# Up-projection matmuls that read and write their 512 token columns in short alternating runs

## The chip, the cores and the metric

The kernel runs on one core of a Trainium2 chip. The metric is the device time of one execution in microseconds (us). Before the change, three timed runs gave a median of 1272.12 us (1269.15 to 1272.39).

## The reference, cut to what matters

Two layers of a small transformer trunk on 512 tokens with a model width of 1024. Layer 0 has stick-breaking attention, layer 1 forgetting attention, each with 16 heads of 64. Each layer ends in a gated channel mixer with 2 x 2816 hidden columns, and that is where the change lies. All arithmetic is float32:

```python
def conv_ffn(x, w_up, conv_w, conv_b, w_down):
    hdn = x @ w_up                                  # (512, 1024) @ (1024, 5632)
    hdn = lax.conv_general_dilated(                 # causal, depthwise, width 3, along the tokens
        hdn, conv_w[:, None, :], window_strides=(1,), padding=[(CONV_WIDTH - 1, 0)],
        dimension_numbers=('NWC', 'WIO', 'NWC'), feature_group_count=2 * D_FF) + conv_b
    gate, up = jnp.split(hdn, 2, axis=-1)
    return (jax.nn.gelu(gate, approximate=True) * up) @ w_down
...
    f = conv_ffn(rmsnorm(h, ffn_pre_g[layer]), w_up[layer], conv_w[layer],
                 conv_b[layer], w_down[layer])
    h = h + rmsnorm(f, ffn_post_g[layer])
```

## The kernel before, in words

**The number format.** Every float32 operand is split into a high part in TensorE's reduced float32 format (`hi`, `AH`) and the remainder (`lo`, `AL`). A product is three matmuls: high by high, high weights by low activations, low weights by high activations.

**Weights.** All weights come as tiles of 512 KB, in the order of one list, `stream`. `make` (L130 to L149) loads a tile by a DMA from SyncE's queue, rounds it on ScalarE (L144) and subtracts on VectorE in two halves (L148). `take` hands out the next tile and keeps `NW` = 8 tiles made ahead.

**The up-projection.** The normalised activations stand transposed in `AH` and `AL`: 128 partitions, 8 blocks of model columns (`KT`), 512 tokens. The 2816 hidden columns are 22 chunks (`NC`) of 128. For each chunk `c` the function `up` (inside `ffn_phase`) computes two products, the gate's half and the linear half, into the two banks of `pair_of(c)`, one of four pairs of PSUM banks. Each product is one call of `w_stationary`: 8 blocks x 3 matmuls = 24 matmuls that add into one bank, the weight tile as the stationary operand, 128 x 512 tokens as the moving one (L213). A chunk thus is 48 matmuls on TensorE.

**Order.** The first three chunks (`EARLY` = 3) run in two halves of 256 tokens each. Chunks 3 to 21 run one after the other with all 512 tokens, `up(c)` and then `gate(c)`. `gate` evacuates both banks: ScalarE's first term of the convolution, VectorE's two further terms (L589), the GELU on ScalarE (L594) and the product on VectorE (L595). After chunk 21 the down-projection (L513) follows. `w_stationary` serves the q, k and gate projections of the attention stages too, with the same line number. The order on the engines is made by the tile framework's scheduler when the program is built.

**Other lines that the rows below name.** All operands of TensorE's moving side and all its outputs are single stretches of columns in this kernel. Some VectorE operations are not. L662 and L666, once each in the set-up, reduce a 128 x 128 identity: L662 sums 16 groups of 8 elements that lie 16 elements apart (64 bytes), so each read is a jump; L666 sums 4 groups, each of 2 runs of 16 elements. L397 (`project_v`) reads PSUM in runs of 128 columns and writes runs of 64 with gaps of 64. L430 (a row maximum in the second attention) and L465 (a difference of a PSUM tile and its rounded copy) go through stretches without a gap.

The loop of a layer, and the matmul at its heart:

```python
for k in range(KT):
    for a, b in ((hi, AH), (hi, AL), (lo, AH)):
        nc.tensor.matmul(ps, a[:, k, :m], b[:, k, t0:t1], start=i == 0, stop=i == n - 1)
...
for c in range(EARLY, NC):
    up(c, (take(), take()), 0, T)
    gate(c)
```

Of the kernel before, what the change touches and what calls it, by code (L numbers as in the profile page):

```python
# [14 lines left out]
P = 128  # L15
T = 512
D = 1024
KT = D // P
# [7 lines left out]
NEG = -1.0e30  # L26
GUARD = 2.0**60
NW = 8
EARLY = 3
POOL_ROWS = (1, 5, 7)  # L30
FILL = (4, 5)
# [6 lines left out]
def f32(ap):  # L38
    return ap.bitcast(F32)
# [3 lines left out]
def tile_trunk(  # L43
# [22 lines left out]
    nc = tc.nc  # L66
# [12 lines left out]
    def pair_of(i):  # L79
        b = PAIRS[i % 4]  # L80
        return PS[:, b : b + 2, :]

    def bank(kind):
        b = {"pj": 4, "zt": 6}[kind] + turn[kind] % 2
        turn[kind] += 1
        return PS[:, b, :]
# [16 lines left out]
    AH = const.tile([P, KT, T], F32R, name="AH")  # L103
    AL = const.tile([P, KT, T], F32R, name="AL")
# [24 lines left out]
    def make(i):  # L129
        src, nk, n, g, eng = stream[i]  # L130
        raw = wp.tile([P, nk, n], F32, name=f"raw{i}", tag="raw", bufs=2)
        hi = wp.tile([P, nk, n], F32R, name=f"whi{i}", tag="whi", bufs=NW)
        lo = wp.tile([P, nk, n], F32R, name=f"wlo{i}", tag="wlo", bufs=NW)
        nc.sync.dma_start(raw, src)
# [19 lines left out]
    def ahead(n):  # L154
        while nmade[0] < min(len(stream), n):
            make(nmade[0])
            nmade[0] += 1

    def take():
        i = nused[0]  # L160
        nused[0] += 1
        ahead(i + NW)
        return made.pop(i)
# [32 lines left out]
    def act_table(name):  # L196
        with ExitStack() as stack:
            for i in users[-8:]:
                stack.enter_context(tc.issue_after(i))
            ld = nc.scalar.preload_act_table_set(name)  # L200
        return tc.issue_after(ins(ld))

    def uses_table(i):
        users.append(ins(i))


    def w_stationary(ps, w, t0=0, t1=T, m=P):
        hi, lo = w
        n = 3 * KT
        i = 0  # L210
        for k in range(KT):
            for a, b in ((hi, AH), (hi, AL), (lo, AH)):
                nc.tensor.matmul(ps, a[:, k, :m], b[:, k, t0:t1], start=i == 0, stop=i == n - 1)  # L213
                i += 1
# [8 lines left out]
    def pre_block(b, g, t4, junk):  # L223

        ss = small.tile([P, 4], F32, name="ss")
        nc.scalar.activation(junk, H[:, b, :], AF.Square, accum_out=ss[:, 0:1])  # L226
        r = rstd_of(ss)
        if g is None:
            nc.scalar.activation(t4, H[:, b, :], AF.Copy, scale=r)
        else:  # L230
            nc.vector.scalar_tensor_tensor(out=t4, in0=H[:, b, :], scalar=r, in1=g, op0=ALU.mult, op1=ALU.mult)  # L231
        ps = pair_of(b).rearrange("p a (k c) -> p (a k) c", c=P)
        for k in range(KT):
            nc.tensor.transpose(ps[:, k, :], t4[:, k * P : (k + 1) * P], ident)  # L234
        sl = slice(b * P, (b + 1) * P)
        nc.scalar.copy(AH[:, :, sl], ps)
        nc.vector.tensor_tensor(out=AL[:, :, sl], in0=ps, in1=f32(AH[:, :, sl]), op=ALU.subtract)

    def post_block(b, y, g, t4, junk):

        ss = small.tile([P, 4], F32, name="ss")
        nc.scalar.activation(junk, y, AF.Square, accum_out=ss[:, 0:1])  # L242
        nc.vector.tensor_tensor(out=t4, in0=y, in1=g, op=ALU.mult)  # L243
        r = rstd_of(ss)
        nc.vector.scalar_tensor_tensor(  # L245
            out=H[:, b, :], in0=t4, scalar=r, in1=H[:, b, :], op0=ALU.mult, op1=ALU.add
        )
# [19 lines left out]
    def gain(pool, g):  # L267
        t = pool.tile([P, D], F32, name="g", tag="g", bufs=2)
        nc.sync.dma_start(t, g.rearrange("(o d) -> o d", o=1).broadcast_to([P, D]))
        return t  # L270


    class Attn:
# [19 lines left out]
        def gates(self):  # L293
# [17 lines left out]
            for t0 in (0, T // 2):  # L311
                w_stationary(ps[:, t0 : t0 + T // 2], ws, t0, t0 + T // 2)
# [206 lines left out]
    def flat_pair(i):  # L519
        return pair_of(i).rearrange("p a c -> p (a c)")  # L520

    def out_proj(done, heads_end):

        w = {}
        after = []
        one = [(1, k) for k in range(KT)]
        order = [(0, k) for k in range(KT - 2)] + one[: FILL[0]] + [(0, KT - 2), heads_end[0]]
        order += one[FILL[0] : FILL[1]] + [heads_end[1]] + one[FILL[1] :]
        order += [(0, KT - 1)] + [(b, k) for b in (2, 3) for k in range(KT)]
        for step in order:  # L530
            if not isinstance(step, tuple):
                after.append(step)
                continue
            b, k = step
            if k not in w:
                w[k] = take()
            with ExitStack() as stack:
                for i in after:
                    stack.enter_context(tc.issue_after(i))
                after = [unit(b, k, KT, (AH[:, k, :], AL[:, k, :]), w[k])]  # L540
            if k == KT - 1:
                done(b)
# [19 lines left out]
    def ffn_phase(l, heads_end, post_g, next_g, final):  # L562
        with tc.tile_pool(name=f"ffn{l}", bufs=2) as pool:
            g1 = gain(pool, post_g)
            g2 = gain(pool, ffn_pre_g[l])
            junk = pool.tile([P, D], mybir.dt.bfloat16, name="junk", bufs=1)

            def mixed(b):
                t4 = pool.tile([P, D], F32, name="t4", tag="t4", bufs=3)
                post_block(b, flat_pair(b), g1, t4, junk)  # L570
                pre_block(b, g2, t4, junk)

            out_proj(mixed, heads_end)
            act = pool.tile([P, NC, T], F32, name="act", bufs=1)

            def up(c, w, t0, t1):
                for i in range(2):
                    w_stationary(pair_of(c)[:, i, t0:t1], w[i], t0, t1)

            def gate(c):  # L580
                y = pair_of(c)
                hc2 = pool.tile([P, 2, T], F32, name="hc", tag="t4", bufs=3)
                hs = []
                for i in range(2):
                    col = cw[:, l, :].rearrange("p (w c) -> p w c", w=4)[:, :, i * NC + c]
                    hc = hc2[:, i, :]
                    nc.scalar.activation(hc, y[:, i, :], AF.Identity, scale=col[:, 2:3], bias=col[:, 3:4])
                    for s in (1, 2):
                        nc.vector.scalar_tensor_tensor(  # L589
                            out=hc[:, s:], in0=y[:, i, : T - s], scalar=col[:, 2 - s : 3 - s], in1=hc[:, s:],  # L590
                            op0=ALU.mult, op1=ALU.add,
                        )
                    hs.append(hc)
                uses_table(nc.scalar.activation(hs[0], hs[0], AF.Gelu_apprx_tanh))  # L594
                nc.vector.tensor_tensor(out=act[:, c, :], in0=hs[0], in1=hs[1], op=ALU.mult)  # L595

            with act_table("gelu_apprx_tanh_and_others"):
                ws = [(take(), take()) for _ in range(EARLY)]
                for t0 in (0, T // 2):
                    for c in range(EARLY):  # L600
                        up(c, ws[c], t0, t0 + T // 2)
                for c in range(EARLY):
# [5 lines that stand above are left out]
            def lhs(k):  # L608
                ah = pool.tile([P, T], F32R, name="ah", bufs=4)
                al = pool.tile([P, T], F32R, name="al", bufs=4)  # L610
                nc.scalar.copy(ah, act[:, k, :])  # L611
                nc.vector.tensor_tensor(out=al, in0=act[:, k, :], in1=f32(ah), op=ALU.subtract)  # L612
                return ah, al

            g3 = gain(pool, ffn_post_g[l])

            def fed(b):
                t4 = pool.tile([P, D], F32, name="t4", tag="t4", bufs=3)
                if final and b == NB - 1:
                    finish(b, pair_of(b), g3, t4, junk)  # L620
                    return
                post_block(b, flat_pair(b), g3, t4, junk)
                if final:
                    nc.sync.dma_start(of[:, b, :], H[:, b, :])
                else:
                    pre_block(b, next_g, t4, junk)

            down_proj(lhs, fed, final)


    with tc.tile_pool(name="pre", bufs=2) as pool:
# [12 lines left out]
        for l in range(2):  # L644
            rows = [conv_w[l, w].rearrange("(c p) -> c p", p=P) for w in range(3)]
            rows.append(conv_b[l].rearrange("(c p) -> c p", p=P))
            for i in range(2):
# [3 lines left out]
                ps = bank("zt")[:, : 2 * nb]  # L651
# [5 lines left out]
        ps = bank("zt")[:, : 2 * KT]  # L657
# [53 lines left out]
```

## Time and profile before

| what | value |
|---|---|
| median of three timed runs | 1272.12 us (1269.15 to 1272.39) |
| the profiled execution's own time | 1275.83 us |
| its span, first to last instruction | 1274.1 us |
| TensorE busy | 1234.1 us, 97% of the span, 6485 matmuls |
| TensorE weight loads busy | 1062.4 us, 83% |
| VectorE busy | 810.5 us, 64% |
| ScalarE busy | 644.7 us, 51% |
| GpSimd busy | 101.7 us, 8% |
| mean granted TensorE clock | 0.991 of full speed |
| DMA | 111.97 MB, mean 88 GB/s |

"Busy" is the share of the span in which an engine had an instruction in flight. Matmuls are pipelined and the profile models their ends, so one matmul's duration overlaps the next one's; what a matmul costs in a stream is the distance from its start to the next start. Weight loads are listed apart from matmuls and run beside them.

### The profile page before, as it was taken

Reading aid. Unit: us, or ns where it says so; the run is one execution under the profiler, and the core shown is the slowest. Engines: PE = TensorE matmul, PEld = TensorE weight load, DVE = VectorE, ACT = ScalarE, POOL = GpSimd, SP = SyncE. Lnnn points to the kernel's source line nnn. Section 1 sums busy time; section 2 is a strip of 40 time slices with the busy share of each in tenths; the row PEclk is TensorE's granted clock in tenths of the full one; section 3 lists DMA queues with packets and bytes.
Section 4 is the critical chain, followed back from the end, with each engine's and each line's share of the span. In section 5 each row is a group of like instructions: output and inputs, shape, how many; then the busy total and the mean of one; then the engine's idle time right before and its main releaser. Section 6 shows DMA issues by size and latency. Waiting matters only on the chain. (4 is left out here: it accounts for less than half of the span.)

```text
span 1274.1 us, 16820 instructions
## 1 busy us (share of the span) xinstructions
PE 1234.1 (97%) x6485; PEld 1062.4 (83%) x6485; DVE 810.5 (64%) x1304; ACT 644.7 (51%) x1085; POOL 101.7 (8%) x163
## 2 busy tenths in 40 slices
PE   6999998999999999999999999999999999999998
PEld 6888886789888888888888988977898888888886
DVE  6899898676655555433477887774775555554323
ACT  5767677445433333323488787664554333333221
POOL 1000003020000000000001222341100000000001
PEclk9999999999999999999999999999999999999999
DMA  6421212034333333333233122110443333333311
GB/s 215 139 66 51 66 50 67 25 90 143 107 99 99 99 93 93 97 99 100 67 81 88 50 83 67 50 50 34 146 120 100 99 99 99 94 93 96 99 34 66
DMA packets 145928, 111.97 MB, mean 88 GB/s; under 512 B 4680, under 2 KB 136120, under 8 KB 145848
## 3 DMA queue, kind: packets, MB, share of 16 engines
q1 hardware_dynamic: 145848, 110.90, 29.4%
q8 instruction: 51, 0.84, 0.3%
q14 instruction: 29, 0.24, 0.1%
HBM read 108.79 MB, written 2.10 MB: 87 GB/s over the span
## 5 line engine op out<-in xcount | busy, mean ns | idle before, releaser
L213 PE MATMUL PS<-AH,whi 128*128 128x512 f32 (+1 forms) x1088 | 398.8, 367 | 4.3 <-DVE QS L362 2.8
L213 PE MATMUL PS<-AL,whi 128*128 128x512 f32 (+1 forms) x1088 | 398.0, 366 | 0.0
L213 PE MATMUL PS<-AH,wlo 128*128 128x512 f32 (+1 forms) x1088 | 397.8, 366 | 0.0
L148 DVE TENSOR_TENSOR wlo<-raw,whi 128x512 fp32r<-128x512 f32 x332 | 217.4, 697 | 211.7 <-ACT whi L144 211.0
L144 ACT CAST whi<-raw 128x1024 fp32r<-128x1024 f32 x172 | 180.8, 1052 | 223.5 <-PE PS L213 177.7
L213 PEld LDWEIGHTS PS<-AH,whi 128*128 128x128 f32 x1088 | 205.6, 189 | 37.2 <-DVE QS L362 3.4
L213 PEld LDWEIGHTS PS<-AL,whi 128*128 128x128 f32 x1088 | 205.8, 189 | 31.8
L213 PEld LDWEIGHTS PS<-AH,wlo 128*128 128x128 f32 x1088 | 205.8, 189 | 31.8
L589 DVE SCALAR_TENSOR_TENSOR hc<-PS,cw,hc 128x511 f32<-128x511 f32 (+1 forms) x176 | 130.7, 745 | 2.7
L513 PE MATMUL PS<-whi,ah 128*128 128x512 f32 x352 | 109.4, 389 | 0.0
L513 PE MATMUL PS<-wlo,ah 128*128 128x512 f32 x352 | 109.4, 389 | 0.0
L513 PE MATMUL PS<-whi,al 128*128 128x512 f32 x352 | 109.4, 389 | 0.0
L612 DVE TENSOR_TENSOR al<-act,ah 128x512 fp32r<-128x512 f32 x44 | 30.4, 690 | 117.2 <-ACT ah L611 117.2
L611 ACT CAST ah<-act 128x512 fp32r<-128x512 f32 x44 | 27.4, 622 | 144.3 <-PE PS L513 138.2
L391 PE MATMUL PS<-whi,AH 128*128 128x256 f32 x256 | 74.9, 293 | 3.9 <-DVE QS L362 1.6
L513 PEld LDWEIGHTS PS<-wlo,ah 128*128 128x128 f32 x352 | 66.1, 188 | 13.8
L513 PEld LDWEIGHTS PS<-whi,ah 128*128 128x128 f32 x352 | 66.1, 188 | 13.7
L219 POOL TENSOR_SCALAR ss<-ss 128x1 f32<-128x1 f32 x31 | 11.9, 385 | 821.0 <-ACT junk L242 755.2
L513 PEld LDWEIGHTS PS<-whi,al 128*128 128x128 f32 x352 | 66.1, 188 | 13.6
L391 PE MATMUL PS<-wlo,AH 128*128 128x256 f32 x256 | 74.6, 291 | 0.0
L391 PE MATMUL PS<-whi,AL 128*128 128x256 f32 x256 | 74.2, 290 | 0.0
L594 ACT ACTIVATE hc<-hc 128x512 f32<-128x512 f32 x44 | 27.8, 631 | 86.8 <-DVE hc L589 86.8
(130 smaller groups left out, 1766.3 us busy)
## 6 DMA issues: line engine op xcount, KB each, us to landing
raw<-w_up_dram SPq DMA_DIRECT2D x88, 512.0 KB
raw<-w_down_dram SPq DMA_DIRECT2D x44, 512.0 KB
raw<-sb_w_qkv_dram SPq DMA_DIRECT2D x24, 512.0 KB
raw<-w_kvf_dram SPq DMA_DIRECT2D x16, 512.0 KB
raw<-sb_w_o_dram SPq DMA_DIRECT2D x8, 512.0 KB
raw<-fox_w_q_dram SPq DMA_DIRECT2D x8, 512.0 KB
raw<-fox_w_o_dram SPq DMA_DIRECT2D x8, 512.0 KB
H<-x_dram SPq DMA_DIRECT2D x4, 512.0 KB
```

The lines of the kernel that those rows point to most:

```text
L144: nc.scalar.copy(hi, raw)
L148: eng.tensor_tensor(out=fl[:, s], in0=fr[:, s], in1=fh[:, s], op=ALU.subtract)
L213: nc.tensor.matmul(ps, a[:, k, :m], b[:, k, t0:t1], start=i == 0, stop=i == n - 1)
L219: nc.gpsimd.tensor_scalar(ss[:, 2:3], ss[:, 0:1], 1.0 / D, EPS, op0=ALU.mult, op1=ALU.add)
L391: nc.tensor.matmul(ps[:, o], a[:, k, sl], m[:, k % 4, :], start=i == 0, stop=i == 3 * KT - 1)
L513: mm = nc.tensor.matmul(y[:, c, :], s[:, sl], m[:, 0, c * 512 : (c + 1) * 512], start=k == 0 and i == 0, stop=k == n - 1 and i == 2,)
L589: nc.vector.scalar_tensor_tensor(out=hc[:, s:], in0=y[:, i, : T - s], scalar=col[:, 2 - s : 3 - s], in1=hc[:, s:], op0=ALU.mult, op1=ALU.add,)
L594: uses_table(nc.scalar.activation(hs[0], hs[0], AF.Gelu_apprx_tanh))
L611: nc.scalar.copy(ah, act[:, k, :])
L612: nc.vector.tensor_tensor(out=al, in0=act[:, k, :], in1=f32(ah), op=ALU.subtract)
```

## The change

For chunks 3 to 21 of both layers, a matmul of the up-projection goes through its 512 token columns in another order. The columns 0 to 255 and 256 to 511 are the two halves. `woven` makes a view that takes `run` columns of the first half, `run` columns of the second, the next `run` of the first, and so on. The same view is put on the moving operand and on the output in PSUM, so each token's result lands where it stood before. The run depends on the chunk's number modulo 8:

| chunk mod 8 | 0 | 1 | 2 | 3 | 4 | 5 | 6 | 7 |
|---|---|---|---|---|---|---|---|---|
| run, columns | none (as before) | 128 | 64 | 32 | 16 | 8 | 4 | 2 |
| chunks | 8, 16 | 9, 17 | 10, 18 | 3, 11, 19 | 4, 12, 20 | 5, 13, 21 | 6, 14 | 7, 15 |
| matmuls in both layers | 192 | 192 | 192 | 288 | 288 | 288 | 192 | 192 |
| runs in one matmul | 1 | 4 | 8 | 16 | 32 | 64 | 128 | 256 |

No instruction is added, taken away or moved: the order on all five engines, the waits among them and the number of instructions are those of the kernel before, and TensorE's list differs in the shape of 1632 matmuls alone (a matmul of chunk 3 is 128x8x2x32 where it was 128x512).

```diff
+RUNS = (None, 128, 64, 32, 16, 8, 4, 2)
...
-    def w_stationary(ps, w, t0=0, t1=T, m=P):
+    def woven(ap, run):
+
+        return ap.rearrange("p (h j c) -> p j h c", h=2, c=run)
+
+    def w_stationary(ps, w, t0=0, t1=T, m=P, run=None):
         hi, lo = w
+        if run:
+            n = 3 * KT
+            i = 0
+            for k in range(KT):
+                for a, b in ((hi, AH), (hi, AL), (lo, AH)):
+                    nc.tensor.matmul(
+                        woven(ps, run), a[:, k, :m], woven(b[:, k, t0:t1], run), start=i == 0, stop=i == n - 1
+                    )
+                    i += 1
+            return
...
             def up(c, w, t0, t1):
                 for i in range(2):
-                    w_stationary(pair_of(c)[:, i, t0:t1], w[i], t0, t1)
+                    run = RUNS[c % len(RUNS)] if c >= EARLY else None
+                    w_stationary(pair_of(c)[:, i, t0:t1], w[i], t0, t1, run=run)
```

## Rows read from the trace of the kernel before

**Rows 1.** The page's first part: busy time, share of the span, instructions.
```profile
PE 1234.1 (97%) x6485; PEld 1062.4 (83%) x6485; DVE 810.5 (64%) x1304; ACT 644.7 (51%) x1085; POOL 101.7 (8%) x163
```

**Rows 2.** Busy time by stretch, up-projections of both layers; then clock, DMA share, GB/s.
```profile
310.00:420.00 110.00, 110.00 (x508) 91.97 (x508) 68.05 (x103) 46.70 (x59) 0.00 (x0) 1.00 0.37 106
420.00:523.00 103.00, 103.00 (x456) 85.31 (x455) 57.25 (x85) 39.67 (x49) 0.00 (x0) 1.00 0.33 97
930.00:1040.00 110.00, 110.00 (x532) 93.03 (x531) 69.58 (x105) 48.15 (x61) 0.00 (x0) 1.00 0.38 110
1040.00:1149.00 109.00, 109.00 (x482) 90.28 (x481) 60.98 (x90) 41.09 (x51) 0.00 (x0) 1.00 0.33 97
```

**Rows 3.** Waits from 315 to 523 us, all engines, the whole list.
```profile
DVE wlo L148 <- ACT whi L144: 81.9, 37, 2.7
ACT whi L144 <- PE PS L213: 78.2, 34, 3.7
ACT hc L594 <- DVE hc L589: 43.2, 20, 2.6
ACT ah L611 <- DVE act L595: 3.1, 2, 2.8
DVE al L612 <- ACT ah L611: 0.7, 1, 0.7
ACT whi L144 <- DMA raw<-w_up_dram: 0.5, 1, 0.5
```

**Rows 4.** TensorE in order of time (start, us, line): the 512-column matmuls' edges, both layers.
```profile
315.22 0.40 PE L213 MATMUL PS<-AH,whi 128*128 128x512 f32 x1
...
521.97 0.62 PE L513 MATMUL PS<-whi,ah 128*128 128x512 f32 x2
...
941.38 0.40 PE L213 MATMUL PS<-AH,whi 128*128 128x512 f32 x1
...
1148.12 0.62 PE L513 MATMUL PS<-whi,ah 128*128 128x512 f32 x2
```

**Rows 5.** The same view among the halves of 256 columns, 36 matmuls, first and last.
```profile
301.78 0.28 PE L213 MATMUL PS<-AH,wlo 128*128 128x256 f32 x1
...
305.98 0.28 PE L213 MATMUL PS<-AL,whi 128*128 128x256 f32 x1
```

**Rows 6.** Groups on VectorE, shapes apart: busy us, mean ns; reads or writes with jumps.
```profile
L662 DVE TENSOR_REDUCE dsel<-ident 128x16 f32<-128x128 f32 x1 | 0.4, 365 | 0.7 <-POOL ident masks.py:199 0.7
L666 DVE TENSOR_REDUCE rows<-ident 128x4 f32<-128x128 f32 x1 | 0.3, 274 | 0.0
L397 DVE TENSOR_TENSOR V<-PS,V 128x256 fp32r<-128x256 f32 x24 | 10.0, 417 | 1.2 <-ACT V L396 1.0
```

**Rows 7.** The same view: the like operations on operands without jumps.
```profile
L430 DVE TENSOR_REDUCE st<-PS 128x1 f32<-128x512 f32 x16 | 10.9, 679 | 0.1
L430 DVE TENSOR_REDUCE st<-PS 128x1 f32<-128x128 f32 x16 | 4.5, 283 | 0.6 <-ACT ec L431 0.4
L465 DVE TENSOR_TENSOR PL<-PS,PH 128x256 fp32r<-128x256 f32 x32 | 13.3, 416 | 3.7 <-ACT PH L464 3.5
```

## The prediction

> **What bounds the kernel now.** I read the page's busy shares first: TensorE has an instruction in flight for 1234.1 of 1274.1 us, 97%, VectorE for 64%, ScalarE for 51% [rows 1]. That is a mean over stages, so the next view is the busy time of the up-projections alone, since no other stage changes. In both layers TensorE is busy for the whole of each stretch (110.00 of 110.00 us and so on) at full granted clock, VectorE for 56 to 63% of it, ScalarE for 38 to 44%, the DMA engines for about a third [rows 2]. The list of waits tells the same from the other side: in layer 0's stretch no wait of TensorE is listed at all, the longest totals being VectorE behind ScalarE (81.9 us) and ScalarE's weight rounding behind the matmuls that free its buffers (78.2 us); behind a weight DMA it waits 0.5 us [rows 3]. So the other engines have slack here and TensorE has none. A nanosecond on an up-projection's matmul is a nanosecond on the end, one for one, and nothing else in the stage can hide it.
>
> What does such a matmul cost? Its listed duration of 0.40 us is no price, since matmuls overlap. The distance of starts is one. The 512-column matmuls of chunks 3 to 21 begin at 315.22 us and the down-projection's first at 521.97; between them lie 19 chunks x 48 = 912 matmuls, so one takes 206.75 / 912 = 226.7 ns. Layer 1 gives (1148.12 - 941.38) / 912 = 226.7 ns [rows 4]. The 256-column matmuls of the early halves are 35 steps in 305.98 - 301.78 = 4.20 us, 120.0 ns each [rows 5]. The difference is 106.7 ns for 256 columns, or **0.417 ns per column**; 512 of them are 213.4 ns, which leaves 13.3 ns per matmul that doesn't depend on the columns. [...]
>
> **The change part by part.** It adds, removes and moves no instruction, no wait and no DMA, so there is one kind of term: the extra time of a matmul whose 512 columns come in runs. There are 1632 of these. 192 each have runs of 128, 64, 4 and 2 columns; 288 each have runs of 32, 16 and 8. The 192 matmuls of chunks 8 and 16 stay as they are. The first three chunks, the projections and the down-projection stay too.
>
> No matmul of this kernel has ever read or written with a jump, so the trace holds no row for the price. The nearest rows are VectorE's. Without jumps a reduction takes 283 ns for 128 columns and 679 for 512, which is 396 / 384 = 1.03 ns per column [rows 7]. The reduction in runs of 16 takes 274 ns for 128 columns, and the one where each of the 128 reads is a jump takes 365 [rows 6]. Runs of 16 cost nothing there, while single jumps cost 82 / 128 = 0.64 ns each. That 16 results are written instead of one may be part of it, but hardly all, since four results cost nothing. A read with a jump then takes 1.03 + 0.64 = **1.67 ns**. For writes there is a row as well: the subtraction that reads PSUM in runs of 128 and writes runs of 64 takes 417 ns for 256 columns, the one without jumps 416 [rows 6, 7].
>
> I carry this over as a floor: a stretch, however short, occupies the read for 1.67 ns. This is a choice, as VectorE is slower and may have another path to the memory. On TensorE a run of c columns streams in 0.417 c ns:
> - Runs of 128, 64, 32, 16 and 8 stream in 53 to 3.3 ns each, above the floor. Cost 0.
> - Runs of 4 stream in 4 x 0.417 = 1.67 ns, exactly the floor. Cost 0, with no margin.
> - Runs of 2 stream in 0.83 ns and would take 1.67. Each matmul has 256 of them, so it loses 256 x 0.83 = 213 ns: its streaming time doubles, from 226.7 to about 440 ns. 192 matmuls x 213.4 ns = **41.0 us**.
>
> The bounds of this term: from below 0, if TensorE fetches ahead far enough. In between, if a jump adds 0.64 ns on top, as VectorE's did, instead of setting a floor: 256 x 0.64 x 192 = 31.5 us. [...]
>
> What the delay does around it: chunks 7 and 15 of each layer grow from 48 x 226.7 ns = 10.9 us to about 21.1. Their evacuation comes later by as much, and VectorE and ScalarE, busy little more than half of the time, wait longer. The weight tiles get further ahead, but TensorE didn't wait for those, so nothing is given back. **Sum:** the profiled execution's own 1275.8 us would become 1316.8; the median of the runs is 3.7 us (0.3%) below that execution, so against it I predict 1272.1 + 41.0 = 1313.1 us.
>
> **The rivals.**
>
> *Runs cost nothing at all (ends on the other side, not slower).* The mechanism: TensorE's read side works on requests that are in flight together, or keeps the two lines between which it alternates, so that each pair of columns is at hand when its tick comes. Its place is again chunks 7 and 15; the point from which it decides is whether a new stretch can be had every 0.83 ns. For it: TensorE holds its rate to the tick over 912 matmuls [rows 4] while weight loads are in flight for 83% of the span [rows 1] and VectorE and ScalarE work on the same memory, so the memory serves several readers without disturbing it. Against it: VectorE, which needs far less per nanosecond, shows a price for jumps [rows 6, 7]. It gives 1272.1 us. [...]
>
> *Each jump costs a bubble.* If going from one run to the next loses one tick of 0.417 ns, every length pays. The runs are 192 x (4 + 8 + 128 + 256) + 288 x (16 + 32 + 64) = 108,288, and x 0.417 ns that is 45.2 us: 1317.3 us. Against it speaks the reduction in runs of 16, whose 8 runs cost nothing [rows 6]. In the profile it would differ from my forecast by chunks 6 and 14 (runs of 4), which would lose 53 ns per matmul.
>
> *Anything but one stretch halves the rate.* If the output in PSUM, which is added to at each tick, is written at full rate only in one stretch, all 1632 matmuls lose 213.4 ns: 348.3 us, 1620.4 us. The nearest row against it: VectorE reads PSUM in runs of 128 for 417 ns and without jumps for 416 [rows 6, 7], though that is no matmul's write. [...] No run here shows a matmul's write either way.
>
> **How the numbers follow.** The floor on a stretch: 0.46. No cost: 0.36. A bubble per jump: 0.08. Half rate for all: 0.05. Some other loss, such as at runs of 4 as well: 0.03. A gain, from nothing that I can name: 0.02. The floor is likeliest because the one row with short jumps shows a price and gives the size; it isn't far ahead, because that row is another engine's and a single instruction. A measurement of this kernel can tell 0.3% (about 4 us) from no change, so faster has 0.02, same 0.36, slower 0.46 + 0.08 + 0.05 + 0.03 = 0.62. The forecast's own range is 1300 to 1317 us (31.5 to 41.0 us, and the spread of runs). The range over the cases must take in no cost and the bubble: 1267 us, which is 0.4% below the median, to 1320 us. It leaves out the half rate for all and part of the other losses.
>
> **What would show it.** In the profile after, TensorE's starts inside chunks 7 and 15 should stand about 440 ns apart and those of all other chunks, 6 and 14 among them, 226.7 ns as now; these four chunks should take 21 us each instead of 10.9, and TensorE should list no new wait. Equal distances in all chunks would make the forecast wrong and the no-cost rival right. A distance that grows by the number of runs would be the bubble. A higher distance already in chunks 9 and 17, with runs of 128, would be the half rate.

## The result and the profile after

The changed kernel takes 1308.82 us (median of four runs, 1307.78 to 1315.60) against 1272.26 us before (four runs), a ratio of 1.0288 with a 95% interval of 1.0264 to 1.0311: **slower by 36.6 us, 2.9%**.

The first part of the page after, against [rows 1]: TensorE still has work in flight for 97% of a span that is 1306.0 us now.

```profile
PE 1267.8 (97%) x6485; PEld 1062.5 (81%) x6485; DVE 810.8 (62%) x1304; ACT 645.6 (49%) x1085; POOL 101.8 (8%) x163
```

Busy time by stretch, with the columns of [rows 2]: the two stages of chunks 3 to 21, both at full granted clock, TensorE without a gap.

```profile
313.10:538.80 225.70, 225.70 (x915) 173.07 (x914) 121.24 (x180) 82.86 (x104) 0.00 (x0) 1.00 0.30 92
954.30:1180.00 225.70, 225.70 (x915) 173.09 (x914) 120.53 (x179) 80.73 (x101) 0.00 (x0) 1.00 0.32 92
```

The waits from 313 to 539 us, against [rows 3], begin with these rows. TensorE's matmuls are again in none of them; the other engines wait a little longer for it.

```profile
DVE wlo L150 <- ACT whi L146: 100.5, 37, 5.4
ACT whi L146 <- PE PS L220: 86.4, 31, 6.3
```

TensorE in order of time, against [rows 4]: the first matmul of chunks 3 to 11 in layer 0, and the first of the down-projection. L220 is a matmul with runs, L229 one without.

```profile
313.11 0.40 PE L220 MATMUL PS<-AH,whi 128*128 128x512 f32 x1
324.46 0.40 PE L220 MATMUL PS<-AH,whi 128*128 128x512 f32 x1
335.98 0.40 PE L220 MATMUL PS<-AH,whi 128*128 128x512 f32 x1
347.66 0.43 PE L220 MATMUL PS<-AH,whi 128*128 128x512 f32 x1
359.68 0.51 PE L220 MATMUL PS<-AH,whi 128*128 128x512 f32 x1
375.99 0.41 PE L229 MATMUL PS<-AH,whi 128*128 128x512 f32 x1
386.90 0.39 PE L220 MATMUL PS<-AH,whi 128*128 128x512 f32 x1
397.78 0.39 PE L220 MATMUL PS<-AH,whi 128*128 128x512 f32 x1
408.66 0.40 PE L220 MATMUL PS<-AH,whi 128*128 128x512 f32 x1
...
538.78 0.63 PE L529 MATMUL PS<-whi,ah 128*128 128x512 f32 x2
```

A chunk is 48 matmuls, so the distance from row to row, divided by 48, is the price of a matmul with that chunk's run. Chunk 7 took 375.99 - 359.68 = 16.31 us, 340 ns per matmul. All chunks with the same run agree within 0.3 ns, in both layers:

| run | none | 128 | 64 | 32 | 16 | 8 | 4 | 2 |
|---|---|---|---|---|---|---|---|---|
| ns per matmul | 227.3 | 226.7 | 226.7 | 236.6 | 240.0 | 243.3 | 250.4 | 339.8 |
| extra over 226.7 | 0 | 0 | 0 | 10.0 | 13.3 | 16.6 | 23.7 | 113 |

(The 0.6 ns of the chunks without runs are the first matmuls behind a run of 2.) The extras sum to 192 x 113 = 21.7 us for the runs of 2, 192 x 23.7 = 4.6 us for the runs of 4 and 288 x (10.0 + 13.3 + 16.6) = 11.5 us for the longer ones, **37.8 us**. The stages agree: 538.78 - 313.11 = 225.67 us where it was 206.75, and the same in layer 1, 18.9 us each. The profiled spans differ by less, 31.9 us. The other 6 us lie outside the two stages, in parts that the change doesn't touch: 2.1 us ahead of the first stage, 3.9 us between the two, in an execution whose mean granted clock was 0.995 where it was 0.991.

### The profile page after: what moved, and what is told of

The parts are those of the page before. It is cut to its first block, busy times and chain, and to the rows that moved or that the text cites. A ratio compares the mean times of both kernels' runs of the same rounds, so it can differ in the third digit from the quotient of the medians.

```text
span 1306.0 us, 16820 instructions
## 1 busy us (share of the span) xinstructions
PE 1267.8 (97%) x6485; PEld 1062.5 (81%) x6485; DVE 810.8 (62%) x1304; ACT 645.6 (49%) x1085; POOL 101.8 (8%) x163
## 4 chain that ended last, share of the span: by engine, by line
PE 71%; DVE 3%; ACT 3%; DMA 2%; issue 1%; POOL 0%; DVEq 0%; POOLq 0%; ACTq 0%; SPq 0%
PE PS L220 31%; PE PS L529 19%; PE PS L229 13%; PE PS L407 3%; PE PS L486 2%; DMA raw<-w_up_dram 1%; PE PS L427 1%; PE PS L474 1%; ACT whi L140 1%; DVE wlo L150 1%; DVE t L247 0%; DVE H L261 0%; ACT junk L242 0%; DVE t L259 0%; DMA raw<-fox_w_q_dram 0%
## 5 line engine op out<-in xcount | busy, mean ns | idle before, releaser
L220 PE MATMUL PS<-AH,whi 128*128 128x512 f32 x544 | 225.1, 414 | 0.0
L220 PE MATMUL PS<-AL,whi 128*128 128x512 f32 x544 | 225.1, 414 | 0.0
L220 PE MATMUL PS<-AH,wlo 128*128 128x512 f32 x544 | 225.1, 414 | 0.0
L229 PE MATMUL PS<-AH,whi 128*128 128x512 f32 (+1 forms) x544 | 186.6, 343 | 3.8 <-DVE QS L378 2.5
L229 PE MATMUL PS<-AL,whi 128*128 128x512 f32 (+1 forms) x544 | 185.7, 341 | 0.0
L229 PE MATMUL PS<-AH,wlo 128*128 128x512 f32 (+1 forms) x544 | 185.5, 341 | 0.0
L220 PEld LDWEIGHTS PS<-AH,wlo 128*128 128x128 f32 x544 | 103.4, 190 | 32.7 <-issue 0.6
L220 PEld LDWEIGHTS PS<-AH,whi 128*128 128x128 f32 x544 | 103.3, 190 | 32.0
L220 PEld LDWEIGHTS PS<-AL,whi 128*128 128x128 f32 x544 | 103.3, 190 | 32.0
L229 PEld LDWEIGHTS PS<-AH,whi 128*128 128x128 f32 x544 | 103.4, 190 | 15.6 <-DVE QS L378 3.2
L229 PEld LDWEIGHTS PS<-AL,whi 128*128 128x128 f32 x544 | 103.4, 190 | 10.7
L229 PEld LDWEIGHTS PS<-AH,wlo 128*128 128x128 f32 x544 | 103.2, 190 | 10.8
```

Source lines behind the costliest of these rows:

```text
L220: nc.tensor.matmul(woven(ps, run), a[:, k, :m], woven(b[:, k, t0:t1], run), start=i == 0, stop=i == n - 1)
```

## The experiments

Unless said otherwise the edits are made to the changed kernel, and each kernel ran once where no ratio is given. A matmul's price is the distance from a chunk's first matmul to the next chunk's, divided by 48 (by 96 where a chunk has 256-column matmuls).

**Reading or writing?** Two kernels put the runs on one side only.

```diff
-                        woven(ps, run), a[:, k, :m], woven(b[:, k, t0:t1], run), start=i == 0, stop=i == n - 1
+                        ps, a[:, k, :m], woven(b[:, k, t0:t1], run), start=i == 0, stop=i == n - 1
```

> This kernel puts the runs on the moving operand alone; the output in PSUM is one stretch, so the tokens of a chunk land in another order and the result is not the reference's. With runs on both sides the distances of starts were 226.7 ns (runs of 128 and 64), 236.7 (32), 240 (16), 243 (8), 250 (4) and 340 (2). Theory READ (all of the loss is in reading the moving operand): the same six distances, and the up-projection stage of a layer stays 18.9 us longer than before the change. Theory WRITE (all of it is in adding to PSUM): 226.7 ns in every chunk, the stage as before the change. Theory EACH (every jump of either side has its own price): something between, say half of each extra.

Read alone, chunk 7 begins and ends at these places:

```profile
361.19 0.51 PE L220 MATMUL PS<-AH,whi 128*128 128x512 f32 x1
377.50 0.41 PE L229 MATMUL PS<-AH,whi 128*128 128x512 f32 x1
```

That is 16.31 us, 340 ns again, and every other chunk has its price of the table above, to 0.2 ns. The time was 1310.3 us against 1273.1 for the kernel before on that chip.

```diff
-                        woven(ps, run), a[:, k, :m], woven(b[:, k, t0:t1], run), start=i == 0, stop=i == n - 1
+                        woven(ps, run), a[:, k, :m], b[:, k, t0:t1], start=i == 0, stop=i == n - 1
```

> The runs on the output in PSUM alone, the moving operand in one stretch; tokens land in another order, so the result is not the reference's. Theory READ: 226.7 ns in every chunk. Theory WRITE: 226.7, 226.7, 236.7, 240, 243, 250 and 340 ns for runs of 128 down to 2. Theory EACH: the remaining half of each extra.

Written alone, chunk 7:

```profile
357.69 0.39 PE L220 MATMUL PS<-AH,whi 128*128 128x512 f32 x1
368.57 0.39 PE L229 MATMUL PS<-AH,whi 128*128 128x512 f32 x1
```

10.88 us, 226.7 ns, as in one stretch, and so in all 19 chunks of the layer (226.6 to 227.2 ns); 1271.1 us in all. Theory READ holds whole: **adding to PSUM in runs down to 2 costs nothing, reading the moving operand in them costs everything.** Writes of single columns weren't tried.

**Once per matmul, or per jump?**

```diff
-RUNS = (None, 128, 64, 32, 16, 8, 4, 2)
+RUNS = (None, None, 64, 32, 16, 8, 4, 2)
...
-                    up(c, (take(), take()), 0, T)
+                    w = (take(), take())
+                    up(c, w, 0, T // 2)
+                    up(c, w, T // 2, T)
```

> Chunks 3 to 21 run as two calls of 256 columns, each with runs from the two halves of its 256 (128 columns apart); chunks with a run of 128 get none, since that is one stretch here. A plain matmul of 256 columns takes 120.0 ns. Theory FIXED (the extra of runs of 32 to 4 is paid once per matmul, at its start): the extras of 10, 13, 17 and 24 ns stay, so 130, 133, 137 and 144 ns for runs of 32, 16, 8 and 4. Theory JUMPS (the extra goes with the number of runs or columns): they halve, to 125, 127, 128 and 132 ns. For runs of 2 FIXED has no say; by JUMPS the 113 ns become 57, so 177 ns. If the distance of the halves in memory matters (512 bytes here, 1024 before), the run of 2 falls off this line.

The first matmuls of chunks 3, 4, 5, 6, 7 and 8 (runs of 32, 16, 8, 4, 2, none):

```profile
313.89 0.28 PE L220 MATMUL PS<-AH,whi 128*128 128x256 f32 x1
325.31 0.28 PE L220 MATMUL PS<-AH,whi 128*128 128x256 f32 x1
336.83 0.29 PE L220 MATMUL PS<-AH,whi 128*128 128x256 f32 x1
348.67 0.29 PE L220 MATMUL PS<-AH,whi 128*128 128x256 f32 x1
361.04 0.33 PE L220 MATMUL PS<-AH,whi 128*128 128x256 f32 x1
377.03 0.30 PE L229 MATMUL PS<-AH,whi 128*128 128x256 f32 x1
```

119.0, 120.0, 123.3, 128.9 and 166.6 ns, where plain is 120.0. Neither theory: the extras of long runs don't stay and don't halve, they vanish (-1 and 0), those of 8 and 4 fall to 3.3 and 8.9, and only that of runs of 2, 46.6, is a little under half of 113. Since the halves are both shorter and closer together in memory, another kernel kept the length of 256 and put the streams 1024 bytes apart, as in the change.

```diff
-    def woven(ap, run):
-        return ap.rearrange("p (h j c) -> p j h c", h=2, c=run)
+    def woven(ap, run, part):
+        v = ap.rearrange("p (h j c) -> p j h c", h=2, c=run)
+        n = v.shape[1] // 2
+        return v[:, part * n : (part + 1) * n]
...
+                    for part in range(2):
+                        for i in range(2):
+                            if run:
+                                w_stationary(pair_of(c)[:, i, :], w[i], 0, T, run=run, part=part)
...
```

> Chunks 3 to 21 in two calls of 256 columns as in the kernel with halves, but each call takes 128 columns from either half of the tokens, so the streams are 1024 bytes apart as in the change, where the kernel with halves had 512. A plain call takes 120 ns; that kernel measured 119, 120, 123, 129 and 167 ns for runs of 32, 16, 8, 4 and 2. If the small extras of runs of 32 to 4 in the change (10, 13, 17 and 24 ns) come from the 1024 bytes, they are seen here too, half or whole: 125 to 130, 127 to 133, 128 to 137, 132 to 144 ns. If they come from the length of 512 columns, the distances are those of the kernel with halves.

The chunks 7 and 8 begin at:

```profile
363.08 0.33 PE L221 MATMUL PS<-AH,whi 128*128 128x256 f32 x1
379.07 0.30 PE L231 MATMUL PS<-AH,whi 128*128 128x256 f32 x1
```

166.6 ns again, and 119.0, 120.0, 123.3 and 128.7 for the others: the distances of the kernel with halves to 0.2 ns. So for 256 columns from two streams the distance between the streams (512 or 1024 bytes) has no part in it; the length of the matmul has. Why 512 columns in runs of 32 lose 10 ns and twice 256 lose none stays open.

**Jumps, places or lines?** More streams, on both sides:

```diff
...
-        return ap.rearrange("p (h j c) -> p j h c", h=2, c=run)
+        c, h = run
+        return ap.rearrange("p (h j c) -> p j h c", h=h, c=c)
...
-                    run = RUNS[c % len(RUNS)] if c >= EARLY else None
+                    run = RUNS[c - EARLY] if c >= EARLY else None
```

> Each of the chunks 3 to 21 has a pair (run, streams): the 512 columns are cut into 2, 4, 8, 32, 64 or 128 equal streams, and a run is taken from each in turn, on both sides. Successive runs then start 1024, 512, 256, 64, 32 or 16 bytes apart; the number of runs in a matmul depends on the run alone. Theory JUMP (each change of run has its price, wherever it goes): all chunks with one run length cost the same, 236.7 ns for 32, 243 for 8, 250 for 4, 340 for 2. Theory BANK (places 512 or 1024 bytes apart get in each other's way): the extra is there with 2 and 4 streams and gone, 226.7 to 230 ns, with 32 streams and more, runs of 2 included. Theory LINE (a memory line of 16 bytes is read anew for each visit, and a run of 2 uses half of it): runs of 2 take 340 ns with any number of streams, even with 128, where the lines are neighbours; of longer runs it says nothing.

Chunks 11 to 16, runs of 2 from 2, 4, 8, 32, 64 and 128 streams, then chunk 17:

```profile
404.12 0.50 PE L223 MATMUL PS<-AH,whi 128*128 128x512 f32 x1
420.12 0.64 PE L223 MATMUL PS<-AH,whi 128*128 128x512 f32 x1
441.42 0.68 PE L223 MATMUL PS<-AH,whi 128*128 128x512 f32 x1
464.79 0.62 PE L223 MATMUL PS<-AH,whi 128*128 128x512 f32 x1
485.50 0.64 PE L223 MATMUL PS<-AH,whi 128*128 128x512 f32 x1
507.64 0.63 PE L223 MATMUL PS<-AH,whi 128*128 128x512 f32 x1
529.30 0.43 PE L223 MATMUL PS<-AH,whi 128*128 128x512 f32 x1
```

| run | 2 streams | 4 | 8 | 32 | 64 | 128 |
|---|---|---|---|---|---|---|
| 2 | 333 | 444 | 487 | 431 | 461 | 451 |
| 4 | 250 | 268 | 278 | 227 | 233 | |
| 8 | 243 | 231 | 234 | 233 | | |
| 32 | 237 | 234 | 237 | | | |

All three theories miss. With four streams and more a run of 2 takes 431 to 487 ns. The streaming part doubled would be 213.4 x 2 + 13.3 = 440 ns, so these run at about **half rate**, neighbouring lines included, which BANK excluded; and the change's two streams were the mild case. The number of jumps is the same in a row of the table, so JUMP falls too. The same order, runs of 2 from two streams, took 340 ns in the change, 333 here and 329 in the next two kernels; why is open, and it is the scatter that a price of this order carries from kernel to kernel.

The second kernel read the moving operand in orders that part the number of jumps from the number of lines:

```diff
-                        woven(ps, run), a[:, k, :m], woven(b[:, k, t0:t1], run), start=i == 0, stop=i == n - 1
+                        view(ps, w_), a[:, k, :m], view(b[:, k, t0:t1], r), start=i == 0, stop=i == n - 1
...
+    def view(ap, how):
+        kind, n, off, size = how
+        ap = ap[:, off : off + size]
...
+            return ap.rearrange("p (j s) -> p s j", s=n)
...
```

> The moving operand alone is read in other orders; the output is one stretch, so tokens land in another order, and where only 496 or 504 columns are read, the last tokens of a chunk are left out. By LINE a run of 2 takes (340 - 13) / 256 = 1.28 ns per visit to a line: then a step of 2 columns takes 340 ns, steps of 4, 8 and 16 and runs of 1 take 512 x 1.28 + 13 = 667 ns, runs of 4 that begin 2 columns off a line (two lines each) cost as much as runs of 2, 335 ns for 504 columns against 247 on the line, runs of 8 off by 2 take 3 lines, 250 ns for 496 columns against 236, and runs of 2 off by 1 about 495 ns. By JUMP steps have no jump and take 227 ns each, runs off the line cost what runs on it cost, and runs of 1 take over 450 ns. One stretch of 504 columns, begun on a line or off it, takes 223 ns by both. Runs of 2 from 4 or 8 streams take 340 ns by both.

Chunks 4 to 8 (steps of 2, 4 and 16; single columns from two streams; then the next chunk):

```profile
324.25 0.61 PE L262 MATMUL PS<-AH,whi 128*128 128x512 f32 x1
345.99 0.64 PE L262 MATMUL PS<-AH,whi 128*128 128x512 f32 x1
368.13 0.61 PE L262 MATMUL PS<-AH,whi 128*128 128x512 f32 x1
388.93 0.40 PE L262 MATMUL PS<-AH,whi 128*128 128x512 f32 x1
399.31 0.41 PE L262 MATMUL PS<-AH,whi 128*128 128x504 f32 x1
```

| read order | LINE | JUMP | measured, ns |
|---|---|---|---|
| step of 2 columns | 340 | 227 | 453 |
| steps of 4, 8, 16 | 667 | 227 | 461, 431, 433 |
| single columns, two streams | 667 | over 450 | **216** |
| runs of 4, on the line / 2 off (504 columns) | 247 / 335 | 247 / 247 | 240 / 325 |
| runs of 8, on the line / 2 off (496 columns) | 236 / 250 | 236 / 236 | 234 / 337 |
| runs of 2, on the line / 1 off (504 columns) | 335 / 495 | 335 / 335 | 323 / 324 |
| runs of 2 from 4 / 8 streams | 340 / 340 | 340 / 340 | 443 / 487 |
| one stretch of 504, on the line / 1 off | 223 / 223 | 223 / 223 | 227 / 227 |

JUMP is finished: steps, which by it have no jump, run at half rate, single columns, which by it jump 512 times, are the fastest, and the same runs moved 2 columns off a multiple of 16 bytes lose 85 to 103 ns (325 against 240, 337 against 234). The 16 bytes were LINE's assumption; these rows show that such a place matters, and no more is meant by a line below. LINE is wrong on the count: a step of 16 with one column per line takes 433 ns, a step of 2 takes 453. Runs of 2 from 4 and 8 streams cost on the read side alone what they cost on both, so the writes were free there too. One stretch of 504 columns takes as long as one of 512, which neither theory gave. And single columns taken in turn from two streams, the order that looks worst, are **10.5 ns faster than one stretch**.

**A theory that fits in part, tried on new orders.** Suppose that the columns are read two at a time, the even and the odd ones of the read order each by a path of its own, and that a path wants two reads in a row from one line. One stretch gives each path two. Runs of 4 on a line do as well. Runs of 2, steps, and runs of 4 begun 2 columns off the line give it one: half rate. Single columns from two streams give it four. Steps and runs of 2 from four and more streams do run at about half rate; but from two streams runs of 2 take 329 to 340 ns and the runs of 4 off the line 325, where half rate would be about 440 and 433, and the extras of 4 to 51 ns of longer runs in the table above the theory doesn't give at all.

```diff
+        if kind == "pairs":
+            return ap.rearrange("p (g h j) -> p g j h", h=2, j=n)
...
```

> Read orders again, on the moving operand alone (output in one stretch, tokens in another order or left out, so not the reference's). Theory PATHS: the even and the odd columns of the order in which they are read go through two read paths, and each path wants two reads in a row from one 16-byte line, else it runs at half rate; with four in a row (single columns from two streams, 216 ns before) it even saves the 10.5 ns. So pairs of single columns from two streams take 216 ns at every distance from 256 down to 4 columns; at a distance of 2 each path has two hits per line, as in one stretch, 227 ns; single columns from 4 streams give each path two streams in turn, as runs of 2 from two streams do, 330 ns; from 8 and 16 streams 440 ns. Pairs 251 columns apart, where the two streams are not at the same place of a line, take 212 ns for 502 columns. For 384 columns, one stretch takes 173 ns and pairs 163. Theory FAR: the 216 ns come from the 1024 bytes between the streams; then pairs lose it as the distance falls, and at 4 and 2 columns, within one or two lines, they take 227 ns. Theory COUNT (what counts is how often a line is left): single columns from 4, 8 and 16 streams all take 216 or all 440 ns.

Chunks 10 to 15 (pairs 4 and 2 columns apart, single columns from 4, 8 and 16 streams, then the next chunk):

```profile
387.06 0.38 PE L264 MATMUL PS<-AH,whi 128*128 128x512 f32 x1
397.43 0.39 PE L264 MATMUL PS<-AH,whi 128*128 128x512 f32 x1
408.35 0.44 PE L264 MATMUL PS<-AH,whi 128*128 128x512 f32 x1
421.91 0.72 PE L264 MATMUL PS<-AH,whi 128*128 128x512 f32 x1
445.35 0.61 PE L264 MATMUL PS<-AH,whi 128*128 128x512 f32 x1
466.15 0.39 PE L264 MATMUL PS<-AH,whi 128*128 128x502 f32 x1
```

Pairs take 215.8 ns at each of the seven distances from 256 down to 4 columns, and 227.5 ns at a distance of 2, where by the model a path is back at two reads in a row: PATHS, and not FAR. 251 columns apart they take 212.9 for 502 columns; 384 columns take 173.5 in one stretch and 165.6 as pairs begun 2 columns off a line (163 expected). Single columns from 8 and 16 streams take 488 and 433 ns, half rate. One miss: from 4 streams, where by the model each path goes back and forth between two lines, they take 283 ns and not 330; why is open. The two paths are a model that no run shows. What the runs show is that it gave the prices of twelve of thirteen orders (one of them, pairs 256 apart, measured before), ten kinds of pairs within 2% and the single columns from 8 and 16 streams within 11%, that FAR and COUNT didn't, and that it leaves the prices named above open.

**One part of the change alone**, runs of 2 in chunks 7 and 15:

```diff
-RUNS = (None, 128, 64, 32, 16, 8, 4, 2)
+RUNS = (None, None, None, None, None, None, None, 2)
```

> The change with its runs of 2 alone (chunks 7 and 15 of each layer); all other chunks in one stretch. By the distances of starts, 192 matmuls lose 113 ns each, 21.7 us: about 1293.5 us, 1.7% over the kernel before. The forecast's floor, 213 ns each, would give 41.0 us, 1313 us.

1296.04 us (four runs) against 1274.41, ratio 1.0174 (1.0147 to 1.0201): 22 us more, as the distances said, and not the floor's 41; chunk 7:

```profile
356.98 0.50 PE L220 MATMUL PS<-AH,whi 128*128 128x512 f32 x1
373.28 0.41 PE L229 MATMUL PS<-AH,whi 128*128 128x512 f32 x1
```

**A version that beats both.** If pairs are faster than one stretch, data that are stored for pairs should make a faster kernel. To the kernel before:

```diff
+        ah, al = AH[:, :, sl], AL[:, :, sl]
+        if pairs:
+            ps = ps.rearrange("p k (j h) -> p k h j", h=2)
+            ah, al = (t.rearrange("p k (h j) -> p k h j", h=2) for t in (ah, al))
...
+                    mv = mv.rearrange("p (b h j) -> p b j h", h=2, j=P // 2)
...
+            r = r.rearrange("p (c j h) -> p c h j", c=2, h=2)
+            h, l = (t.rearrange("p (c h j) -> p c h j", c=2, h=2) for t in (h, l))
+            nc.scalar.copy(h, r)
...
-                    y[:, c, :], s[:, sl], m[:, 0, c * 512 : (c + 1) * 512],
+                    y[:, c, :], s[:, sl], m[:, 0, c * 512 : (c + 1) * 512].rearrange("p (h j) -> p j h", h=2),
```

> The kernel before, with the up-projection's activations and the row weights of the output and down projections stored so that the even columns of a block come first and the odd ones behind them (distance 64 and 256 columns), and read back in turn, one column from each; outputs stay where they were. PATHS: each of the 1824 + 1440 matmuls of 512 columns loses 10.5 ns of its 226.7, the up-projections of a layer take 9.6 us less for chunks 3 to 21 and the whole 34 us less, about 1238 us, with perhaps 3 to 6 us more from the 576 matmuls of 256 columns. FAR: only the 1440 with a distance of 256 columns gain, 15 us, about 1257 us. If VectorE or ScalarE, whose reads now step over every second column, slow down by more than their slack, TensorE waits for weights and the gain is smaller.

1242.52 us (four runs) against 1271.71, ratio **0.9763 (0.9740 to 0.9786)**, near the 1238 of PATHS and not the 1257 of FAR. Chunks 3 to 21 of layer 0 stand between

```profile
317.84 0.38 PE L225 MATMUL PS<-AH,whi 128*128 128x512 f32 x1
...
514.68 0.38 PE L529 MATMUL PS<-whi,ah 128*128 128x512 f32 x1
```

which is 196.84 / 912 = 215.8 ns each, and 256 columns take 111.7 ns at full clock. By these distances 3264 matmuls x 10.9 ns + 576 x 8.3 ns = 40 us should be gained; 29 were. Part of the rest is visible ahead of layer 0's up-projection: TensorE waits 3.3 us for the pre-norm there, which took 1.2 us before. The granted clock, 1.00 before from 290 to 300 us, is 0.56 and then 0.75 there, and matmuls of 256 columns start 213 ns apart until 297.35 us. The end of the wait, then stretches of 5 us (span, TensorE busy, granted clock, DMA share, GB/s):

```profile
291.96 1.97 PE L246 MATMUL PS<-ident,t 128*128 128x128 f32 x8 [3.33 <-DVE t L243]
...
290.00:295.00 5.00, 3.04 (x14) 0.56 0.45 132
295.00:300.00 5.00, 5.00 (x37) 0.75 0.72 210
```

ScalarE also pays for reading every second column of a weight tile: its rounding of a row tile takes 1452 ns in the mean where the others take 1049. That mean mixes two kinds. The tiles of the output projections, made in the attention stages, take 1137 ns in the mean of 8, those of the down-projections, made from the end of the up-projection on, 1575 in the mean of 22. First the other tiles, then the row tiles between 140 and 215 us and between 470 and 590:

```profile
L153 ACT CAST whi<-raw 128x1024 fp32r<-128x1024 f32 x112 | 117.2, 1049 | 170.1 <-PE PS L225 124.1 <-DMA raw<-w_up_dram 31.4 <-DMA raw<-sb_w_qkv_dram 13.5
L148 ACT CAST whi<-raw 128x1024 fp32r<-128x1024 f32 x8 | 9.1, 1137 | 1.6 <-PE PS L225 1.5
L148 ACT CAST whi<-raw 128x1024 fp32r<-128x1024 f32 x22 | 34.7, 1575 | 12.9 <-PE PS L225 12.1 <-DMA raw<-w_down_dram 0.8
```

The operands and shapes are the same, so the step alone doesn't set the price. What does isn't shown: the other tiles, most of them the up-projection's, are read in one stretch and take 1049 ns in the mean.

The last kernel left the output projection's weights in one stretch (in `make`, `if i in woven` for the down-projection's tiles only, instead of `if nk == 1`), to see whether the wait of 3.3 us goes and the clock stays at 1.00.

```diff
-        if nk == 1:
+        if i in woven:
...
-                    y[:, c, :], s[:, sl], m[:, 0, c * 512 : (c + 1) * 512].rearrange("p (h j) -> p j h", h=2),
+                mv = m[:, 0, c * 512 : (c + 1) * 512]
+                if pairs:
+                    mv = mv.rearrange("p (h j) -> p j h", h=2)
```

> The kernel with pairs again, but the output projection's row weights in one stretch as before, so that ScalarE's longer rounding of those tiles (1452 ns against 1052) falls away in front of the up-projection. [...] If the faster output projection is what exposed that wait, it goes back to about 1.2 us and the clock holds; the 384 matmuls lose their 10.9 ns gain, 4.2 us, and the whole comes out within 3 us of 1242.5. If the clock falls at this place for another reason, the whole takes about 1246 us.

1239.70 us (six runs) against 1274.41, ratio 0.9736 (0.9708 to 0.9764); the intervals of the two kernels overlap, so which is better isn't told. The wait came down to 2.0 us, not 1.2, and the granted clock was below 1.00 in one of these stretches (0.66) in place of two:

```profile
289.60 1.09 PE L250 MATMUL PS<-ident,t 128*128 128x128 f32 x8 [1.96 <-DVE t L247]
...
290.00:295.00 5.00, 5.00 (x33) 0.66 0.40 117
295.00:300.00 5.00, 5.00 (x47) 1.00 0.58 167
```

So the pairs in the output projection were part of the cause of the wait, not all of it. From the transposes of the third token block in order to those of the fourth, the chain through the pre-norm takes 12.8 us in the kernel before and in this one, and 14.6 us with pairs everywhere. Of the two things that the edit takes back, the shorter matmuls and the longer roundings of these tiles, the runs don't show which made the chain longer; the roundings, 8 tiles at about 90 ns more each, are done by 211 us. The rest of the wait is plain: TensorE fills the chain's time with 88 matmuls of 256 columns, and these are 88 x 8.3 ns = 0.7 us shorter as pairs, so 1.2 us became 2.0.

## Why the prediction was right, and where not

The forecast was 1313.1 us, 41.0 us more; measured were 36.6 us more, inside the forecast's own range. Point by point:

- **Nothing hides a nanosecond of the up-projection.** Right. The distances sum to 37.8 us, the stages grew by exactly that, and no wait of TensorE's matmuls appeared in the list. The page's 97% didn't change, and couldn't have told.
- **Distances of starts are the price of a matmul, not the listed duration.** Right: the duration of a run of 2 grew from 0.39 to 0.51 us, the price from 227 to 340 ns.
- **Runs of 128 and 64 cost 0.** Right. **Runs of 32, 16, 8 and 4 cost 0.** Wrong: 10.0, 13.3, 16.6 and 23.7 ns, 16.1 us in all. The step that failed is the floor of 1.67 ns per stretch, carried over from one VectorE instruction: it gives no price to runs of 4 and more. The 1.67 was also worked out from unlike rows, a reduction that reads SBUF (365 ns) against one that reads PSUM (283); against the other reduction out of SBUF, 274 ns, a jump would cost 0.71 ns, not 0.64.
- **Runs of 2 double the streaming time, 213 ns.** Mis-sized: 113 ns, 21.7 us in place of 41.0; the part alone measured 22 us. The total came out close because the two errors, 19.3 us too much here and 16.1 too little above, have opposite signs, which is luck. The half rate itself is real, but belongs to steps and to runs of 2 from four and more streams (431 to 487 ns); with two streams runs of 2 lose about half as much.
- **The mechanism**, that a short visit to a place in memory occupies the read for as long as a longer one, was right in that the loss is on the read side and that runs of 2 pay most. A floor per stretch is refuted: stretches of one column from two streams cost less than one long stretch, and runs of 4, of the same length throughout, take 227 to 278 ns by the number of streams. The model that came nearest counts how many reads in a row each of two paths makes on a line; it gave twelve of thirteen prices and isn't shown. The number of columns read in a row from one line doesn't set the price: runs of 2 and steps of 2 columns, both with two, take 340 and 453 ns.
- **The rivals.** No cost: refuted at every run from 32 down (10.0 to 113 ns more). A bubble per jump: refuted, since 512 columns in runs of 4, with 128 jumps each time, take 227 to 278 ns, runs of 2, with 256 jumps, 329 to 487, and single columns from two streams, with a jump at each column, 216. Half rate for anything but one stretch: refuted by the runs of 128 and 64 (226.7 ns) and by the writes alone (226.6 to 227.2 ns).
- **A gain: 0.02, from nothing that I could name.** None of the change's own orders gave one, but single columns from two streams did. The 13.3 ns that I took for independent of the columns are mostly gone with them: 215.8 ns is 2.4 over the 213.4 that I reckoned for 512 columns (about 5 at 256 and 384).

## What to carry to other kernels

For float32 matmuls in the reduced format the order in which the moving operand is read is a price of its own: keep runs of 64 columns or more, or at least runs of 4 that begin on a multiple of 16 bytes (0 to 51 ns more per 512 columns), and avoid steps and runs of 2, which took 102 to 260 ns more, up to the whole streaming time again and somewhat over. Output runs in PSUM, down to pairs of columns, were free (226.6 to 227.2 ns). Where TensorE bounds the kernel, storing the moving operand as even columns, then odd ones, and reading one from each in turn took 11 ns off each matmul of 512 columns (about 5%), 2.4 to 2.6% off this kernel, so long as whoever stores it that way has slack: ScalarE took 1137 and 1575 ns in the mean for the rounding of such a tile, 1049 for the others.

## What the runs showed that was not expected

- An order of single columns from two streams is faster than one stretch (216 against 227 ns for 512 columns, 112 against 120 for 256), at each distance tried from 4 to 256 columns.
- A step of 16 columns costs no more than a step of 2 (433 and 453 ns): about half rate (up to 488 ns) is the worst of all orders tried.
- Extras don't scale with the length: in runs of 32, a matmul of 512 columns loses 10 ns and one of 256 loses none. Why is open.
- ScalarE, reading every second column of a tile in SBUF, took 1137 ns in the mean in one part of the kernel and 1575 in another, in place of about 1050, while its cast of the activations from PSUM in the same step took 1005 ns in place of 1007. Why the two parts differ is open.
